# Adding minus the mean on DVE instead of POOL, and later memory scores, in a two-layer encoder step

## The chip, the cores and the metric

The kernel runs on one core of a Trainium2 chip. Times are microseconds (us) of device time for one launch; the number quoted for a kernel is the median of its runs. The engines are PE (TensorE, the matrix engine), DVE (VectorE), ACT (ScalarE), POOL (GpSimd) and SP (SyncE, which here only issues transfers).

## The reference, cut to what matters

One step of an encoder with two layers, for 256 prompt tokens and 64 sample tokens, 2048 features each, in fp32. Both layers also attend with 4 heads into 256 memory tokens.

```python
def layer_norm(x, g, b):
    mu = jnp.mean(xf, axis=-1, keepdims=True)
    var = jnp.mean(jnp.square(xf - mu), axis=-1, keepdims=True)
    y = (xf - mu) * lax.rsqrt(var + LN_EPS) * g + b

def mem_attend(q, mk, mv):
    s = jnp.einsum('bthd,bmhd->bhtm', q, mk) / math.sqrt(HEAD_DIM)
    p = jax.nn.softmax(s, axis=-1)
    return jnp.einsum('bhtm,bmhd->bthd', p, mv)

for layer in range(DEPTH):
    # layer 0: short convolution; layer 1: stick-breaking attention over one shared K and V
    main = ...
    mo = mem_attend(q_m, mem_k[layer], mem_v[layer])
    mix = jnp.concatenate([main, mo], axis=-1) @ w_out[layer]
    x = layer_norm(ALPHA * x + mix, ln_g[layer, 0], ln_b[layer, 0])
    f = jnp.square(jax.nn.relu(x @ w_ff1[layer])) @ w_ff2[layer]
    x = layer_norm(ALPHA * x + f, ln_g[layer, 1], ln_b[layer, 1])
```

## The kernel before

All 320 tokens lie on the free axis; features lie on the 128 partitions, as 16 feature tiles (`res`, the residual). Each product is made of panels of 256 output features (two tiles of 128). A panel's weights come in chunks of 4 feature tiles by 256 columns (512 KB), over SP's queue, into three buffers `raw`. For nearly full fp32 accuracy each factor is split into a rounded part and a rest: ACT casts `hi`, DVE subtracts `lo` (L126, L127), into five buffers each. PE then runs 24 matmuls for a chunk, three per feature tile and column tile: lo by xh, hi by xl, hi by xh (L172 to L174). `xh` and `xl` are the tokens' two parts. A quarter panel is the 12 matmuls of a chunk and one column tile.

Three of the four layer norms lie between two products: norm 0 before layer 0's feed-forward, norm 1 before layer 1's input product, norm 2 before layer 1's feed-forward. (The fourth, the output's, is written by another function, `write`, which the change leaves alone.) The product that follows such a norm does not wait for the mean and the deviation. Its first gemm, of two panels at once (four tiles, 8 chunks, all four accumulators `acc` in PSUM), runs on un-normalised tokens with two more columns (322 wide), and its four sums are finished afterwards: `finished` (L406 to L414) copies two columns (`wgb`, ACT), adds mneg times wgb (L412, DVE, which reads `acc` and so frees it), and multiplies by rstd (L413). Meanwhile `normalise` (L391 to L404) makes the true normalised tokens for all later gemms, four feature tiles at a time in four turns c0 to c3: add mneg on POOL (L399), multiply by rstd on DVE (L400), scale and shift tile by tile on ACT (L402), then split into `xh` and `xl` (L126, L127). `finish` (L352 to L371) makes mneg (ACT, L361) and, in three DVE instructions, rstd (L369 to L371).

In layer 1 the four tiles of the first gemm are the memory attention's four queries. `in_b` finishes them (L627, L628) and calls `mem_attend`, which puts three stages into a list: scores, turn and values. The stages are run one by one between quarter panels by `tick`; `later` says from which quarter panel on:

```python
    def later(gap, fn):
        stages.append((now[0] + 2, gap, fn))
```

The order on each engine is not simply the program's: a scheduler places instructions of all stages by its own estimate, and each engine then runs its list strictly in order.

Of the kernel before, what the change touches and what calls it, by code (L numbers as in the profile page):

```python
# [14 lines left out]
ALU = mybir.AluOpType  # L15
# [3 lines left out]
DM = 2048          # model width  # L19
KT = DM // P       # feature tiles  # L20
TP, TS = 256, 64   # prompt and sample tokens
T = TP + TS
DFF = 8192
NM = 256           # memory tokens
NMH = 4            # memory heads
DMEM = NMH * P
NH = 12            # main heads / main feature tiles
PAST = 512
CW = 256           # columns of a weight chunk
CK = 4             # feature tiles of a weight chunk  # L30
NKC = KT // CK
AFTER = (2, 3, 4, 5)   # chunks of the next products, after which their factors are normalised
CUTS = (0, 1, CK)   # pieces of the first chunks
# [7 lines left out]
def encoder_step(  # L41
    ctx: ExitStack,
    tc: tile.TileContext,
    xT: bass.AP,       # [P, KT, T]
    memT: bass.AP,     # [NKC, P, CK, NM]
    w_in_a: bass.AP,   # [20, NKC, P, CK, CW]
    w_in_b: bass.AP,
    w_mem: bass.AP,    # [2, 4, NKC, P, CK, CW]
    w_out: bass.AP,    # [2, 8, NKC, P, CK, CW]
    w_ff1: bass.AP,    # [2, 32, NKC, P, CK, CW]  # L50
    w_ff2: bass.AP,    # [2, 8, 4 * NKC, P, CK, CW]
    ck: bass.AP,       # [NH, P, PAST]
    cv: bass.AP,       # [NH, P, 4, P]
    cmk: bass.AP,      # [2, P, NMH, NM]
    cmv: bass.AP,      # [2, P, 2, DMEM]
    conv_w: bass.AP,   # [P, NH, 3]
    state: bass.AP,    # [P, NH, 2]
    ln_g: bass.AP,     # [P, 4, KT]
    ln_b: bass.AP,
    y_out: bass.AP,    # [P, KT, T]  # L60
    conv_out: bass.AP,  # [P, NH, 2, 2]
    k_out: bass.AP,    # [NH, P, T]
    v_out: bass.AP,    # [NH, P, T]
    mk_out: bass.AP,   # [2, NMH, P, NM]
    mv_out: bass.AP,   # [2, 2, P, DMEM]
# [12 lines left out]
    # Exp, Ln and every simple function in one table  # L78
    nc.scalar.preload_act_table_set("natural_log_exp_and_others")

# [8 lines left out]
    # mask[s, t]: 0 where s < t, BIG elsewhere  # L89
# [8 lines left out]
    # ntri[s', s] = -1 where s' >= s  # L98
# [30 lines left out]
    def load_split(jobs, cuts=(0, CK)):  # L129
        """jobs: (source, hi, lo) of chunks; loaded and split up to each cut of their feature tiles in turn."""  # L130
        raws = [wpool.tile([P, CK, CW], F32, name="raw", bufs=3) for _ in jobs]
        for a, b in zip(cuts[:-1], cuts[1:]):
            for raw, (src, hi, lo) in zip(raws, jobs):
                nc.sync.dma_start(out=raw[:, a:b, :], in_=src[:, a:b, :])
            for raw, (src, hi, lo) in zip(raws, jobs):
                split(hi[:, a:b, :], lo[:, a:b, :], raw[:, a:b, :])
# [9 lines left out]
    # stages of attention, run one by one between the products of the next tiles  # L146
# [3 lines left out]
    def later(gap, fn):  # L150
        """fn, at least gap quarter panels after the last stage (and one after this)."""
        stages.append((now[0] + 2, gap, fn))
# [7 lines left out]
    def gemm(panels, ah, al, on_tile, width=T, after=None):  # L160
        """panels: lists of chunk sources, worked on together; on_tile(i, j, psum); after(chunk)."""
        accs = [[pacc.tile([P, 512], F32, name="acc") for _ in range(CW // P)] for _ in panels]
        n = len(panels[0])
        for c in range(n):
            for i, panel in enumerate(panels):
                hi, lo = chunk(panel[c])
                for j in range(CW // P):
                    acc = accs[i][j][:, :width]
                    cols = slice(j * P, (j + 1) * P)
                    for k in range(CK):  # L170
                        kt = c * CK + k
                        mm(acc, lhsT=lo[:, k, cols], rhs=ah[:, kt, :width], start=kt == 0, stop=False)  # L172
                        mm(acc, lhsT=hi[:, k, cols], rhs=al[:, kt, :width], start=False, stop=False)  # L173
                        mm(acc, lhsT=hi[:, k, cols], rhs=ah[:, kt, :width], start=False, stop=kt == n * CK - 1)  # L174
                    if c == n - 1:
                        on_tile(i, j, acc)
                    tick()
            if after:
                after(c)

# [1 line left out]
    def mem_kv(layer, values, between=None):  # L182
        """The keys of the four heads, or the values."""
# [37 lines left out]
    def wk():  # L221
        """The pool of a phase's small tiles, in the place of the last phase's."""
        if phases:
            phases.pop().close()
        phases.append(ExitStack())
        ctx.callback(phases[-1].close)
        return phases[-1].enter_context(tc.tile_pool(name="work", bufs=2))
# [8 lines left out]
    def mem_attend(h, qm, mixh, mixl, turns):  # L236
# [40 lines left out]
        later(1, scores)  # L277
# [4 lines left out]
    class Norm:  # L282
        """Of r = factor * res + the last products, as they come. The next products begin on g * (r - c) (in xh and
        xl, with g and b as two more columns), and their sums are finished with the mean and the deviation."""
# [19 lines left out]
        def add(self, m, acc):  # L304
            """The last product for feature tile m: res[m] * factor + acc."""
            f = self.factor
            if m < 4:
                nc.vector.scalar_tensor_tensor(out=res[:, m, :], in0=res[:, m, :], scalar=f, in1=acc,
                                               op0=ALU.mult, op1=ALU.add)
                if m == 3:  # L310
                    self.center()
                return
            nc.vector.tensor_tensor(out=res[:, m, :], in0=acc, in1=res[:, m, :], op=ALU.add)  # L313
            last = m == KT - 1
            sq = work.tile([P, T], F32, name="sq")
            nc.scalar.activation(sq, res[:, m, :], AF.Square)  # L316
            if not last:
                nc.vector.tensor_tensor(out=self.s1, in0=self.s1, in1=res[:, m, :], op=ALU.add)
                nc.vector.tensor_tensor(out=self.s2, in0=self.s2, in1=sq, op=ALU.add)
            self.ahead(m)  # L320
            if last:
                self.finish(sq)

        def center(self):
            """c: the mean of the first 4 * P features, by which all are shifted."""
# [26 lines left out]
        def finish(self, sq):  # L352
# [10 lines left out]
            # var + eps: the shift keeps the mean below sqrt(3) deviations, so it stays above 0  # L363
# [4 lines left out]
            # one Newton step of 1 / sqrt(var)  # L368
# [6 lines left out]
        def write(self):  # L375
            """The normalised tokens are the result: the tiles shared among the engines."""
# [14 lines left out]
        def normalise(self, _):  # L391
            """Four feature tiles, a while after the first products have had theirs."""
            self.turn += 1
            if self.turn not in AFTER:
                return
            c = AFTER.index(self.turn)
            s = slice(c * CK, (c + 1) * CK)
            r = res[:, s, :]
            nc.gpsimd.tensor_tensor(out=r, in0=r, in1=mneg.unsqueeze(1).to_broadcast([P, CK, T]), op=ALU.add)  # L399
            nc.vector.tensor_tensor(out=r, in0=r, in1=rstd.unsqueeze(1).to_broadcast([P, CK, T]), op=ALU.mult)  # L400
            for m in range(c * CK, (c + 1) * CK):
                nc.scalar.activation(res[:, m, :], res[:, m, :], AF.Identity, bias=lb[:, self.idx, m:m + 1],  # L402
                                     scale=lg[:, self.idx, m:m + 1])
            split(xh[:, s, :T], xl[:, s, :T], r)  # L404

        def finished(self, acc, tag="qT"):  # L406
            """The product with the normalised tokens, without W' b; and W' b."""
# [125 lines left out]
    def stick_z(h, d):  # L533
# [4 lines left out]
        def z():  # L538
            # prompt in (keys 0, tokens 0), (keys 1, tokens 1), (keys 0, tokens 1); sample by key block
# [14 lines left out]
            # n = softplus(z) = max(z, 0) + ln(1 + exp(-|z|))  # L554
# [9 lines left out]
            # sums over the later key blocks of the sample  # L564
# [13 lines left out]
    def stick_a(h, d):  # L578
# [4 lines left out]
        def turn():  # L583
            # values with the keys on the partitions
# [8 lines left out]
        def sums():  # L593
            # log a = z - (sum of n over this key and the later ones)
# [30 lines left out]
    def in_b(m, acc):  # L625
        if m < NMH:
            qm, wb = norm.finished(acc, ("qT", "qT", "npr", "nsm")[m])  # L627
            nc.vector.tensor_scalar(out=qm, in0=qm, scalar1=wb, scalar2=QSCALE, op0=ALU.add, op1=ALU.mult)  # L628
            mem_attend(m, qm, mixh, mixl, 2)
# [30 lines left out]
def _panels(w):  # L660
    """[K, N] -> [N / CW, K / (CK * P), P, CK, CW]"""
    k, n = w.shape
    return np.ascontiguousarray(w.reshape(k // (CK * P), CK, P, n // CW, CW).transpose(3, 0, 2, 1, 4))
# [59 lines left out]
```

## Time and profile before

| what | value |
|---|---|
| median of 3 runs | 2850.72 us (2850.52 to 2853.23) |
| span of the profiled execution, first to last instruction | 2849.1 us |
| PE busy | 2801.0 us, 98% of the span |
| DVE busy | 1443.8 us, 51% |
| ACT busy | 1121.9 us, 39% |
| POOL busy | 86.6 us, 3% |
| granted PE clock, mean | 0.993 of full speed |
| mean traffic | 150 GB/s |

The profiled execution's own time is not listed apart from its span; the three runs lie 1.4 to 4.1 us above that span. A matmul of 320 columns is recorded as 0.31 us long, while the next one starts 0.15 us after it: PE's spans overlap, so its idle time is best read from the distance of two starts. In a timeline a row gives start, duration, engine, line, what is written and read, and in brackets the idle time before it with what ended it.

### The profile page before, as it was taken

What the parts mean: (1) busy time and instruction counts of PE and PEld (TensorE: products, weight loads), DVE (VectorE), ACT (ScalarE), POOL (GpSimd) and SP (SyncE); (2) the same over time, 40 slices, a digit from 0 to 9 for tenths busy, and PEclk for the clock granted to TensorE, in tenths of its full rate; (3) what the DMA queues carried; (4) which work ended last, traced back from release to release, by engine and by line L of the source; (5) the groups of instructions that cost most, each with busy time, mean ns of one, the idle gap of its engine ahead of it and who ended that gap; (6) DMA issues with size and microseconds to landing.
All of it is one profiled execution on the core that took longest, in us unless ns stands there. A gap on an engine that the chain in (4) does not pass through costs nothing.

```text
span 2849.1 us, 45960 instructions
## 1 busy us (share of the span) xinstructions
PE 2801.0 (98%) x19432; PEld 2773.9 (97%) x19432; DVE 1443.8 (51%) x1924; ACT 1121.9 (39%) x1537; POOL 86.6 (3%) x101
## 2 busy tenths in 40 slices
PE   8999999999999999999989999999999999999996
PEld 8999999999999999999989999999999999999996
DVE  5454457744444454445674444566444444444465
ACT  5433334543333243334454444445323333433333
POOL 1000000100000000000010000000000000000001
PEclk9999999999999999999999999999999999999998
DMA  8545555455555454554534545454544554555542
GB/s 295 179 127 148 150 153 149 126 150 154 149 149 150 152 149 148 150 153 142 155 110 150 152 152 157 123 154 137 152 149 148 151 151 149 148 150 152 150 148 89
DMA packets 118111, 427.52 MB, mean 150 GB/s; under 512 B 13761, under 2 KB 14321, under 8 KB 117905
## 3 DMA queue, kind: packets, MB, share of 16 engines
q1 hardware_dynamic: 113904, 412.14, 48.3%
q0 software_dynamic: 4000, 12.45, 1.3%
q8 instruction: 152, 2.49, 0.4%
q14 instruction: 55, 0.44, 0.0%
HBM read 415.86 MB, written 8.68 MB: 149 GB/s over the span
## 4 chain that ended last, share of the span: by engine, by line
PE 96%; DVE 1%; ACT 1%; DMA 1%; issue 0%; SPq 0%; ACTq 0%; DVEq 0%
PE acc L172 30%; PE acc L174 30%; PE acc L173 30%; DMA raw<-w_mem 1%; PE acc L206 1%; PE acc L205 1%; PE acc L204 1%; PE acc L200 0%; PE acc L202 0%; PE acc L201 0%; ACT hi L126 0%; PE zs L243 0%; ACT xh L126 0%; ACT res L402 0%; PE av L616 0%; DVE lo L127 0%
## 5 line engine op out<-in xcount | busy, mean ns | idle before, releaser
L127 DVE TENSOR_TENSOR lo<-raw,hi 128x1024 fp32r<-128x1024 f32 (+1 forms) x769 | 940.6, 1224 | 1209.2 <-ACT hi L126 1207.8
L126 ACT CAST hi<-raw 128x1024 fp32r<-128x1024 f32 (+1 forms) x769 | 805.4, 1047 | 1359.5 <-PE acc L174 1273.3
L172 PE MATMUL acc<-xh,lo 128*128 128x320 f32 (+1 forms) x3328 | 1036.5, 311 | 9.3 <-DVE fin L412 9.3
L174 PE MATMUL acc<-xh,hi 128*128 128x320 f32 (+1 forms) x3328 | 1033.5, 311 | 0.0
L173 PE MATMUL acc<-xl,hi 128*128 128x320 f32 (+1 forms) x3328 | 1029.7, 309 | 0.0
L174 PE MATMUL acc<-mh,hi 128*128 128x320 f32 x2560 | 792.1, 309 | 0.0
L172 PE MATMUL acc<-mh,lo 128*128 128x320 f32 x2560 | 791.3, 309 | 0.0
L173 PE MATMUL acc<-ml,hi 128*128 128x320 f32 x2560 | 791.0, 309 | 0.0
L172 PEld LDWEIGHTS acc<-xh,lo 128*128 128x128 f32 x3328 | 628.0, 189 | 14.0 <-DVE fin L412 10.3
L174 PEld LDWEIGHTS acc<-xh,hi 128*128 128x128 f32 x3328 | 628.5, 189 | 2.5 <-issue 2.3
L173 PEld LDWEIGHTS acc<-xl,hi 128*128 128x128 f32 x3328 | 627.7, 189 | 0.9 <-issue 0.4
L172 PEld LDWEIGHTS acc<-mh,lo 128*128 128x128 f32 x2560 | 480.6, 188 | 0.4
L174 PEld LDWEIGHTS acc<-mh,hi 128*128 128x128 f32 x2560 | 480.6, 188 | 0.3
L173 PEld LDWEIGHTS acc<-ml,hi 128*128 128x128 f32 x2560 | 480.6, 188 | 0.0
L126 ACT CAST mh<-rs 128x320 fp32r<-128x320 f32 x128 | 58.9, 460 | 58.5 <-DVE rs L436 58.4
L127 DVE TENSOR_TENSOR ml<-rs,mh 128x320 fp32r<-128x320 f32 x128 | 62.5, 489 | 31.6 <-ACT mh L126 31.6
L399 POOL TENSOR_TENSOR res<-res,mneg 128x1280 f32<-128x1280 f32 x12 | 37.4, 3142 | 1134.4 <-ACT mneg L361 1134.4
L436 DVE TENSOR_TENSOR rs<-rl 128x320 f32<-128x320 f32 x128 | 62.4, 489 | 8.0 <-ACT rl L434 8.0
L443 DVE SCALAR_TENSOR_TENSOR res<-res,acc 128x320 f32<-128x320 f32 x96 | 46.5, 484 | 39.2 <-PE acc L174 39.2
L434 ACT ACTIVATE rl<-acc 128x320 f32<-128x320 f32 x120 | 52.4, 437 | 32.9 <-PE acc L174 30.7
L200 PE MATMUL acc<-memh,lo 128*128 128x256 f32 x128 | 38.8, 303 | 9.3 <-DVE lo L127 9.3
L316 ACT ACTIVATE sq<-res 128x320 f32<-128x320 f32 x48 | 22.5, 469 | 59.5 <-DVE res L313 59.5
(208 smaller groups left out, 1256.8 us busy)
## 6 DMA issues: line engine op xcount, KB each, us to landing
raw<-w_ff SPq DMA_DIRECT2D x512, 512.0 KB, 3.6
raw<-w_in_a SPq DMA_DIRECT2D x80, 512.0 KB, 3.6
raw<-w_in_b SPq DMA_DIRECT2D x80, 512.0 KB, 3.6
raw<-w_out SPq DMA_DIRECT2D x64, 512.0 KB, 3.6
raw<-w_mem SPq DMA_DIRECT2D x31, 512.0 KB, 4.8
ckT<-ck POOLq DMA_DIRECT2D x12, 256.0 KB, 3.2
cvS<-cv POOLq DMA_DIRECT2D x12, 256.0 KB, 3.3
res<-xT SPq DMA_DIRECT2D x4, 640.0 KB, 6.3
```

The lines of the kernel that those rows point to most:

```text
L126: nc.scalar.copy(hi, src)
L127: nc.vector.tensor_tensor(out=lo, in0=src, in1=hi.bitcast(F32), op=ALU.subtract)
L172: mm(acc, lhsT=lo[:, k, cols], rhs=ah[:, kt, :width], start=kt == 0, stop=False)
L173: mm(acc, lhsT=hi[:, k, cols], rhs=al[:, kt, :width], start=False, stop=False)
L174: mm(acc, lhsT=hi[:, k, cols], rhs=ah[:, kt, :width], start=False, stop=kt == n * CK - 1)
L200: mm(acc, lhsT=wl[:, k, cols], rhs=mh[:, k, :], start=first, stop=False)
L204: mm(acc, lhsT=ml[:, k, cols], rhs=wh[:, k, :], start=first, stop=False)
L205: mm(acc, lhsT=mh[:, k, cols], rhs=wl[:, k, :], start=False, stop=False)
L399: nc.gpsimd.tensor_tensor(out=r, in0=r, in1=mneg.unsqueeze(1).to_broadcast([P, CK, T]), op=ALU.add)
L434: nc.scalar.activation(r, acc, AF.Relu)
L436: nc.vector.tensor_tensor(out=s, in0=r, in1=r, op=ALU.mult)
L443: nc.vector.scalar_tensor_tensor(out=res[:, m, :], in0=res[:, m, :], scalar=ALPHA if g == 0 else 1.0, in1=acc, op0=ALU.mult, op1=ALU.add)
```

## The change

Two edits, and comments removed (which makes no instruction different). In `normalise` the add of mneg is issued on DVE instead of POOL: 4 instructions of 128x1280 elements at each of norms 0, 1 and 2. In `mem_attend` the scores' stage gets a lag of its own, 4 quarter panels in layer 1 instead of 2; layer 0 keeps 2.

```diff
-    def later(gap, fn):
-        stages.append((now[0] + 2, gap, fn))
+    def later(gap, fn, lag=2):
+        stages.append((now[0] + lag, gap, fn))
...
-    def mem_attend(h, qm, mixh, mixl, turns):
+    def mem_attend(h, qm, mixh, mixl, turns, lag=2):
...
-        later(1, scores)
+        later(1, scores, lag)
         later(3, turn)
         later(1, values)
...
             r = res[:, s, :]
-            nc.gpsimd.tensor_tensor(out=r, in0=r, in1=mneg.unsqueeze(1).to_broadcast([P, CK, T]), op=ALU.add)
+            nc.vector.tensor_tensor(out=r, in0=r, in1=mneg.unsqueeze(1).to_broadcast([P, CK, T]), op=ALU.add)
             nc.vector.tensor_tensor(out=r, in0=r, in1=rstd.unsqueeze(1).to_broadcast([P, CK, T]), op=ALU.mult)
...
-            mem_attend(m, qm, mixh, mixl, 2)
+            mem_attend(m, qm, mixh, mixl, 2, 4)
```

DVE's list at norm 0, from the variance on (var, msq and rstd are the norm's; res is the residual; lo a chunk's rest; xl the tokens' rest; fin a finished sum), before:

```order
L364 SCALAR_TENSOR_TENSOR var<-zs,msq 128x320
L369 SCALAR_TENSOR_TENSOR msq<-r_5174 128x320
L370 TENSOR_TENSOR var<-msq,var 128x320
L371 SCALAR_TENSOR_TENSOR rstd<-var,r_5174 128x320
L400 TENSOR_TENSOR res<-res,rstd 128x1280
L127 TENSOR_TENSOR lo<-raw,hi 128x1024
L400 TENSOR_TENSOR res<-res,rstd 128x1280 x2
L127 TENSOR_TENSOR lo<-raw,hi 128x1024
L127 TENSOR_TENSOR xl<-res,xh 128x4x320
L400 TENSOR_TENSOR res<-res,rstd 128x1280
```

and now:

```order
L364 SCALAR_TENSOR_TENSOR var<-zs,msq 128x320
L399 TENSOR_TENSOR res<-res,mneg 128x1280
L369 SCALAR_TENSOR_TENSOR msq<-r_5174 128x320
L399 TENSOR_TENSOR res<-res,mneg 128x1280
L370 TENSOR_TENSOR var<-msq,var 128x320
L399 TENSOR_TENSOR res<-res,mneg 128x1280
L371 SCALAR_TENSOR_TENSOR rstd<-var,r_5174 128x320
L127 TENSOR_TENSOR lo<-raw,hi 128x1024
L400 TENSOR_TENSOR res<-res,rstd 128x1280 x2
L127 TENSOR_TENSOR lo<-raw,hi 128x1024
L400 TENSOR_TENSOR res<-res,rstd 128x1280
L399 TENSOR_TENSOR res<-res,mneg 128x1280
```

Three of the four adds stand between the steps of rstd, and a chunk's lo goes ahead of the first multiplication; the lists of norms 1 and 2 change in the same way up to here.

ACT's list at norm 0, the part that ends with the first copy of wgb (hi a chunk's rounded part, xh the tokens'), before:

```order
L126 CAST xh<-res 128x4x320
L402 ACTIVATE res<-res,lgb 128x320
L126 CAST hi<-raw 128x1024
L402 ACTIVATE res<-res,lgb 128x320 x2
L126 CAST hi<-raw 128x1024
L402 ACTIVATE res<-res,lgb 128x320 x2
L126 CAST xh<-res 128x4x320
L126 CAST hi<-raw 128x1024
L409 COPY wgb<-acc 128x2 x2
```

and now, from the two hi behind Exp on:

```order
L126 CAST hi<-raw 128x1024 x2
L402 ACTIVATE res<-res,lgb 128x320 x5
L126 CAST xh<-res 128x4x320
L402 ACTIVATE res<-res,lgb 128x320 x3
L126 CAST hi<-raw 128x1024
L126 CAST xh<-res 128x4x320
L402 ACTIVATE res<-res,lgb 128x320 x4
L126 CAST hi<-raw 128x1024 x2
L402 ACTIVATE res<-res,lgb 128x320
L126 CAST xh<-res 128x4x320
L402 ACTIVATE res<-res,lgb 128x320
L409 COPY wgb<-acc 128x2
```

The first copy of wgb now stands ahead of the last two scalings, behind 14 of the 16 and behind three casts of xh, as before; before, all 16 stood ahead of it.

PE's list where layer 1's first gemm ends (322 wide) and the next begins (320 wide), with the first memory head's scores (L243; zs, zp are their places in PSUM, fin its finished query, mk_sb and smk the memory keys of prompt and sample), before:

```order
L172 MATMUL acc<-xh,lo 128x322
L243 MATMUL zs<-mk_sb,fin 128x256
L243 MATMUL zp<-mk_sb,fin 128x256
L173 MATMUL acc<-xl,hi 128x322
L174 MATMUL acc<-xh,hi 128x322
L172 MATMUL acc<-xh,lo 128x322
L173 MATMUL acc<-xl,hi 128x322
L174 MATMUL acc<-xh,hi 128x322
L172 MATMUL acc<-xh,lo 128x322
L173 MATMUL acc<-xl,hi 128x322
L174 MATMUL acc<-xh,hi 128x322
L243 MATMUL zs<-smk,fin 64x256
```

and now:

```order
L172 MATMUL acc<-xh,lo 128x322
L173 MATMUL acc<-xl,hi 128x322
L174 MATMUL acc<-xh,hi 128x322
L243 MATMUL zs<-mk_sb,fin 128x256
L243 MATMUL zp<-mk_sb,fin 128x256
L172 MATMUL acc<-xh,lo 128x320
L173 MATMUL acc<-xl,hi 128x320
```

The first two scores stand 8 matmuls later, at the very end of the first gemm; the third, which stood right behind that end, now follows 19 matmuls of the next gemm. SP's list is the same in both.

## Rows read from the trace of the kernel before

**Rows 1.** The page's first lines: span, busy time of each engine.

```profile
span 2849.1 us, 45960 instructions
...
PE 2801.0 (98%) x19432; PEld 2773.9 (97%) x19432; DVE 1443.8 (51%) x1924; ACT 1121.9 (39%) x1537; POOL 86.6 (3%) x101
```

**Rows 2.** PE's waits: who waited for whom, us in total, times, longest.

```profile
PE acc L172 <- DVE fin L412: 9.3, 4, 3.8
...
PE zs L243 <- DVE fin L628: 7.3, 1, 7.3
```

**Rows 3.** Waits of PE's weight loads, same columns.

```profile
PEld zs L243 <- ACT p L248: 1.3, 6, 0.3
```

**Rows 4.** Timeline of PE at the end of norm 0's first gemm.

```profile
548.67 0.30 PE L174 MATMUL acc<-xh,hi 128*128 128x322 f32 x1
552.74 0.41 PE L172 MATMUL acc<-xh,lo 128*128 128x320 f32 x1 [3.77 <-DVE fin L412]
```

**Rows 5.** Timeline of PE near the end of norm 1's first gemm.

```profile
1458.56 0.31 PE L174 MATMUL acc<-xh,hi 128*128 128x322 f32 x1
1458.71 0.32 PE L172 MATMUL acc<-xh,lo 128*128 128x322 f32 x1
```

**Rows 6.** Stretches behind the waits; the third number from the right is PEclk.

```profile
550.00:560.00 10.00, 7.09 (x36) 6.84 (x36) 9.23 (x14) 7.17 (x15) 0.00 (x0) 0.83 0.63 183
1466.30:1476.30 10.00, 9.95 (x46) 8.24 (x47) 7.71 (x19) 4.31 (x13) 0.00 (x0) 0.74 0.35 105
1945.00:1955.00 10.00, 6.63 (x34) 6.63 (x35) 8.96 (x14) 7.18 (x14) 0.00 (x0) 0.83 0.65 199
```

**Rows 7.** Timeline of POOL at norm 0.

```profile
520.73 12.45 POOL L399 TENSOR_TENSOR res<-res,mneg 128x1280 f32<-128x1280 f32 x4 [115.78 <-ACT mneg L361]
```

**Rows 8.** Timeline of DVE from norm 0's variance to its first finished sum.

```profile
520.82 0.48 DVE L364 SCALAR_TENSOR_TENSOR var<-zs,msq 128x320 f32<-128x320 f32 x1
522.35 1.72 DVE L369 SCALAR_TENSOR_TENSOR msq<-r 128x320 f32<-128x320 f32 x1 [1.04 <-ACT r L367]
524.10 3.13 DVE L370 TENSOR_TENSOR var<-msq,var 128x320 f32<-128x320 f32 x1
527.26 3.12 DVE L371 SCALAR_TENSOR_TENSOR rstd<-var,r 128x320 f32<-128x320 f32 x1
530.48 4.06 DVE L400 TENSOR_TENSOR res<-res,rstd 128x1280 f32<-128x1280 f32 x1
...
535.60 2.88 DVE L400 TENSOR_TENSOR res<-res,rstd 128x1280 f32<-128x1280 f32 x2
538.40 1.21 DVE L127 TENSOR_TENSOR lo<-raw,hi 128x1024 fp32r<-128x1024 f32 x1
539.54 1.48 DVE L127 TENSOR_TENSOR xl<-res,xh 128x1280 fp32r<-128x1280 f32 x1
...
552.15 0.54 DVE L412 SCALAR_TENSOR_TENSOR fin<-mneg,wgb,acc 128x320 f32<-128x320 f32 x1
```

**Rows 9.** Timeline of POOL at the last norm (function write).

```profile
2827.33 5.12 POOL L380 TENSOR_TENSOR res<-res,mneg 128x320 f32<-128x320 f32 x5 [898.50 <-ACT mneg L361]
```

**Rows 10.** Timeline of DVE at the last norm.

```profile
2832.72 0.48 DVE L370 TENSOR_TENSOR var<-msq,var 128x320 f32<-128x320 f32 x1
...
2833.52 0.48 DVE L371 SCALAR_TENSOR_TENSOR rstd<-var,r 128x320 f32<-128x320 f32 x1
```

**Rows 11.** Timeline of ACT at norm 0: scalings, casts, first copies of wgb.

```profile
534.57 2.30 ACT L402 ACTIVATE res<-res,lgb 128x320 f32<-128x320 f32 x4 [9.51 <-DVE res L400]
536.78 1.04 ACT L126 CAST hi<-raw 128x1024 fp32r<-128x1024 f32 x1
537.72 1.28 ACT L126 CAST xh<-res 128x1280 fp32r<-128x1280 f32 x1
...
551.56 0.21 ACT L409 COPY wgb<-acc 128x2 f32<-128x2 f32 x2
```

**Rows 12.** Timeline of DVE at norm 1: the first query finished.

```profile
1465.82 0.38 DVE L628 TENSOR_SCALAR fin<-fin,wgb 128x320 f32<-128x320 f32 x1
```

## The prediction

> **What bounds the kernel now.** I read the page's head first: PE is busy for 98% of the span [rows 1], so only what keeps PE waiting or slow can move the time. Next I read PE's waits [rows 2]. Two entries matter: PE's matmuls wait four times, 9.3 us in all, for DVE's finished sums (fin, L412), which free the accumulators, and once, 7.3 us, for the first memory query (fin, L628). The timelines place them: two at norm 0 (the longer is [rows 4]), two alike at norm 2, and the long one at norm 1, when PE stands in front of the first scores, 16 matmuls into the last chunk of the gemm [rows 5]. A start follows a start after 0.15 us in undisturbed work [rows 5], while a matmul is recorded as 0.30 long, so each of the five waits costs some 0.15 more than its entry: 548.67 to 552.74 less 0.15 is 3.92, and the entry is 3.77 [rows 4]. The five waits are 16.6 + 5 x 0.15 = 17.4 us.
>
> They cost more than that, as the windows behind them show [rows 6]: the granted clock averages 0.83 over 10 us behind norm 0's long wait, 0.83 behind norm 2's, and 0.74 behind norm 1's. [...] In all three cases PE had stood still before the clock fell. Waits and clock together: **23.4 us**, all of it at three of the four norms.
>
> **Why DVE and ACT are late there.** At norm 0 POOL's four adds run back to back from 520.73 for 12.45 us, 3.1 each [rows 7]. Beside them DVE's msq takes 1.72, var 3.13, rstd 3.12 and the first multiplication 4.06 us [rows 8]. At the last norm POOL's adds end at 2832.45 [rows 9], and right after it var and rstd take 0.48 each [rows 10], on tiles of the same size. So the long ones are not the price of the work: a DVE instruction that overlaps an add on POOL ends with it, and three small instructions in a row cost three adds. Only the first multiplication needs an add's result at all. From 522.35 to 534.54 DVE does what else would take about 0.5 + 0.5 + 0.5 + 1.4, or 2.9 us: 9 us are lost. ACT pays for it, standing idle for 9.51 us until that multiplication is done [rows 11]; behind it lie 16 scalings and the casts, and so the first wgb comes at 551.56 [rows 11] and fin at 552.15 [rows 8].
>
> **The change, part by part.** *The adds.* POOL loses three times 12.45 us; nothing behind them on POOL is wanted at that time. DVE gains 12 adds. No add of that shape on DVE is in the trace; the nearest rows are L400, the same shape, types and broadcast operand: two in 2.80 us from start to start, 1.40 each, and 1.48 for the longest reading [rows 8]. The bounds are 1.40, and 3.1 if an add cost on DVE what it cost on POOL. I take 1.40: same engine, same bytes.
>
> Now DVE's new list at norm 0, with steps of 0.4 for var and 0.46 for msq and rstd (0.54 less the overlap): variance to 521.2, add c0 522.6, msq 523.1, add c1 524.5, var 524.9, add c2 526.3, rstd 526.7, lo 527.9 (1.14, the step from 538.40 to 539.54 [rows 8]), multiplication c0 529.3, c1 530.7, lo 531.8, c2 533.2, add c3 534.6, xl 536.0, lo 537.2, c3 538.6. Before, c0 was done at 534.5, c1 and c2 by 538.4 [rows 8]. So DVE, although it does 5.6 us more, hands ACT its first work **5.2 us earlier**.
>
> ACT's list from there, with 0.55 for a scaling (2.21 for four), 0.94 for hi and 1.2 for xh [rows 11]: five scalings and xh 533.3, three scalings, hi and xh 537.0, four scalings and two hi 541.1, scaling, xh and scaling 543.4, wgb 543.6. (PE allows that: tile 0's sums end three quarter panels, 36 x 0.15 = 5.4 us, ahead of the end of the gemm at 548.8.) DVE's xl for that xh ends at 544.4, and fin at 544.9. PE asks for the accumulator at 548.8: nearly 4 us to spare. If ACT kept its old list, its 17.0 us from 534.57 to 551.56 would merely start 5.2 earlier: fin ends at 547.5, still in time. The second wait there, for the fourth fin, was at most 0.9 (9.3 less two of 3.8, over two) and goes with the same shift. Norm 2 has the same lists. Gain: 2 x (3.92 + 1.04 + 1.7) = 13.3 us.
>
> *Norm 1.* L628 ended at 1466.2 [rows 12]. By the shift of fin at norm 0 (552.15 to 544.4, 7.7 us) it ends at 1458.5, by DVE's 5.2 alone at 1461.0. PE stood ready at 1458.9 [rows 5].
>
> *The later scores.* PE's work is the same; its first two scores stand 8 matmuls later, so PE asks at 1458.71 + 9 x 0.15 = 1460.1. By the count nothing waits; by the worse bound 0.9 us are left. Of the 10.1 us lost at norm 1 (7.5 waiting, 2.6 by the clock) the adds alone would save 7 to 10, and the later scores at most the last 1.2. What is queued behind the scores on PE is the weights' matmuls; what follows from them is that the softmax, the transposes and the first stick-breaking head come one or two quarter panels later (1.8 us each), beside matmuls of the panels, which don't need them. The one place that can show a new wait is the third score: it takes zs again, which ACT's exponential must have read, and ACT stands there behind xh c3, which itself must wait for the end of the first gemm. Such waits were 1.3 us for six in the kernel before, 0.3 at most [rows 3]; the ends are 0 and 1.3, and I take 0.7.
>
> **Sum.** 23.4 - 0.7 = 22.7 us. From the span of 2849.1 that leaves 2826.4; the median stood 1.6 above that span, so **2828.0 us**.
>
> **Rivals.** *First, the score wait stays in part.* For it: at norm 1 DVE's list puts a chunk's lo and two more sums ahead of the first L628, and each lo waits for its cast. Against it: those casts have their buffers by then. If the query came at 1463.8, PE would wait some 3.8 us and the clock fall as it did behind the 3.8 us of norm 0: 3.8 + 1.7, or 2833.5 us; if nothing at all were gained at norm 1, 2838.1. It decides when L628 ends later than 1460.1.
>
> *Second, slower: the adds lengthen DVE's list.* If DVE's long steps came from something else than POOL (their operands, say), they would stay, and 4 x 1.40 = 5.6 us would come on top, at three norms. For it: DVE was busy for 9.23 of 10 us behind norm 0's wait [rows 6] and POOL for 3% of the span [rows 1], so work goes from an idle engine to the one that is late. The price: 3 x 5.6 = 16.8, and another 1.7 us at half clock behind each, some 5: 2872 us. It decides by whether var (L370) still takes over 3 us with POOL empty; the last norm [rows 9, 10] says no. [...]
>
> *Third, no change:* ACT, not DVE, decides when fin comes, and its 16 scalings and casts take up the 5.2 us. Then the waits stay within a few us of what they are, and the time within 0.2% (5.7 us, about what a measurement can tell from no change): 2848. Against it: ACT's 9.51 us of idle time [rows 11] end with DVE's multiplication.
>
> **Chances.** The forecast 0.80, the first rival 0.13, the second 0.03, the third 0.04. Both of the first are faster by over 0.2%: 0.93 in all; same 0.04; slower 0.03. The range reaches from 2825.5 (no new wait, 2827.3, less 1.8 for the scatter of 2.7 us between runs) to 2838 (nothing gained at norm 1). An add at 3.1 us on DVE would put multiplication c0 at 534.4 instead of 529.3, which is the third rival's place.
>
> **What the changed profile would show.** Right: var and rstd at 0.5 us at norms 0 to 2; POOL's busy time down by 37 us to 49; the adds at 1.4 to 1.5 us; no PE wait on fin over 1 us; the granted clock 1.00 over the three stretches; DVE's busy time down, by 3 x 9 for the stretched steps against 12 x 1.48 added, to about 1435. Wrong: L370 or L371 still near 3 us; PE still waiting for L412 or L628; a new wait of PE on ACT's exponential or on a weight chunk, with the clock falling behind it.

## The result, and the profile after

The changed kernel takes 2827.77 us (median of 4 runs, 2826.41 to 2828.56) against 2850.62 us for the kernel before (4 runs): the ratio is 0.9918, with a 95% interval of 0.9906 to 0.9930. The forecast was 2828.0. The execution profiled took 2827.72 us, 1.7 above its span.

The page's head, where [rows 1] stood before (busy time, share of the span, instructions):

```profile
span 2826.0 us, 45944 instructions
...
PE 2792.7 (99%) x19432; PEld 2767.3 (98%) x19432; DVE 1432.4 (51%) x1936; ACT 1122.9 (40%) x1537; POOL 49.4 (2%) x89
```

DVE, with twelve instructions more, is busy for 11 us less, and POOL for 37 us less. PE's waits, where [rows 2] stood (total, times, longest):

```profile
PE acc L200 <- DVE lo L127: 11.0, 5, 4.7
```

There is no other entry. This one belongs to the start-up and stood in the kernel before too, with 9.3 us; both entries of [rows 2] are gone. Where the time came from is read from one instruction that each norm has once, the variance (L364), in DVE's timeline; first the kernel before, norms 1 and 2 and the output's (norm 0's, at 520.82, is the first of [rows 8]):

```profile
1432.05 0.48 DVE L364 SCALAR_TENSOR_TENSOR var<-zs,msq 128x320 f32<-128x320 f32 x1
...
1916.46 0.48 DVE L364 SCALAR_TENSOR_TENSOR var<-zs,msq 128x320 f32<-128x320 f32 x1
...
2827.10 0.49 DVE L364 SCALAR_TENSOR_TENSOR var<-zs,msq 128x320 f32<-128x320 f32 x1 [1.73 <-PE zs L358]
```

and the changed kernel, from norm 0 on:

```profile
521.09 0.48 DVE L364 SCALAR_TENSOR_TENSOR var<-zs,msq 128x320 f32<-128x320 f32 x1
...
1425.61 0.48 DVE L364 SCALAR_TENSOR_TENSOR var<-zs,msq 128x320 f32<-128x320 f32 x1
...
1900.08 0.48 DVE L364 SCALAR_TENSOR_TENSOR var<-zs,msq 128x320 f32<-128x320 f32 x1
...
2804.00 0.49 DVE L364 SCALAR_TENSOR_TENSOR var<-zs,msq 128x320 f32<-128x320 f32 x1 [1.73 <-PE zs L358]
```

| stretch | before | after | gain |
|---|---|---|---|
| start to norm 0 | 520.82 | 521.09 | -0.3 |
| norm 0 to norm 1 | 911.23 | 904.52 | 6.7 |
| norm 1 to norm 2 | 484.41 | 474.47 | 9.9 |
| norm 2 to the last norm | 910.64 | 903.92 | 6.7 |
| last norm to the end of the span | 22.0 | 22.0 | 0 |

The sum is 23.1 us, the difference of the two spans; the three norms alone make 23.4 (unrounded). The first stretch holds nothing that was changed: up to the same instruction it took from 519.64 to 522.24 us in the runs below whose lists agree up to there, so its -0.3 is scatter. DVE's timeline at norm 0, where [rows 8] stood, shows how:

```profile
521.49 1.48 DVE L399 TENSOR_TENSOR res<-res,mneg 128x1280 f32<-128x1280 f32 x1
522.89 0.48 DVE L369 SCALAR_TENSOR_TENSOR msq<-r 128x320 f32<-128x320 f32 x1
523.29 1.48 DVE L399 TENSOR_TENSOR res<-res,mneg 128x1280 f32<-128x1280 f32 x1
524.70 0.48 DVE L370 TENSOR_TENSOR var<-msq,var 128x320 f32<-128x320 f32 x1
525.10 1.49 DVE L399 TENSOR_TENSOR res<-res,mneg 128x1280 f32<-128x1280 f32 x1
526.50 0.48 DVE L371 SCALAR_TENSOR_TENSOR rstd<-var,r 128x320 f32<-128x320 f32 x1
526.90 1.22 DVE L127 TENSOR_TENSOR lo<-raw,hi 128x1024 fp32r<-128x1024 f32 x1
528.04 2.88 DVE L400 TENSOR_TENSOR res<-res,rstd 128x1280 f32<-128x1280 f32 x2
...
544.89 0.54 DVE L412 SCALAR_TENSOR_TENSOR fin<-mneg,wgb,acc 128x320 f32<-128x320 f32 x1
```

msq, var and rstd take 0.48 us each instead of 1.72, 3.13 and 3.12, and an add on DVE 1.48 (1.40 from start to start). ACT's first scaling and first wgb, where [rows 11] stood:

```profile
529.56 2.84 ACT L402 ACTIVATE res<-res,lgb 128x320 f32<-128x320 f32 x5 [0.66 <-DVE res L400]
...
543.92 0.16 ACT L409 COPY wgb<-acc 128x2 f32<-128x2 f32 x1
```

ACT's idle 9.51 us have become 0.66. The first fin ends at 545.43 (544.89 + 0.54), and PE takes up the next gemm without a break, here in PE's timeline, where [rows 4] stood:

```profile
548.94 0.31 PE L174 MATMUL acc<-xh,hi 128*128 128x322 f32 x1
549.09 0.31 PE L172 MATMUL acc<-xh,lo 128*128 128x320 f32 x1
```

At norm 1 the first query is finished by DVE at 1451.86 + 0.38 (first row; [rows 12] before), and PE reaches the scores at 1453.60, 0.14 us behind the matmul before them (the two rows of its timeline):

```profile
1451.86 0.38 DVE L628 TENSOR_SCALAR fin<-fin,wgb 128x320 f32<-128x320 f32 x1
```

```profile
1453.46 0.30 PE L174 MATMUL acc<-xh,hi 128*128 128x322 f32 x1
1453.60 0.59 PE L243 MATMUL zs<-mk_sb,fin 128*128 128x256 f32 x2
```

The windows behind norms 0, 1 and 2 (same columns as [rows 6]) now show a granted clock of 1.00 throughout:

```profile
550.00:560.00 10.00, 10.00 (x70) 10.00 (x70) 9.55 (x15) 6.50 (x14) 0.00 (x0) 1.00 0.44 128
1453.60:1463.60 10.00, 10.00 (x65) 9.01 (x64) 9.52 (x21) 5.02 (x12) 0.00 (x0) 1.00 0.38 115
1935.00:1945.00 10.00, 10.00 (x70) 10.00 (x70) 5.80 (x7) 3.51 (x4) 0.00 (x0) 1.00 0.69 209
```

In the kernel before, the windows of [rows 6] were made up of stretches at 1.00 and at 0.50, here behind norm 1's wait:

```profile
1468.00:1470.00 2.00, 2.00 (x8) 1.91 (x8) 1.57 (x5) 1.13 (x4) 0.00 (x0) 0.50 0.01 4
...
1472.00:1474.00 2.00, 2.00 (x17) 1.99 (x16) 1.21 (x5) 1.58 (x5) 0.00 (x0) 1.00 0.77 246
```

The waits of PE's weight loads on the memory heads' exponential, where [rows 3] stood:

```profile
PEld zs L243 <- ACT p L248: 1.4, 6, 0.3
```

### The profile page after: what moved, and what is told of

It is laid out like the page before. It is cut to its first block, busy times and chain, and to the rows that moved or that the text cites. A ratio compares the mean times of both kernels' runs of the same rounds, so it can differ in the third digit from the quotient of the medians.

```text
span 2826.0 us, 45944 instructions
## 1 busy us (share of the span) xinstructions
PE 2792.7 (99%) x19432; PEld 2767.3 (98%) x19432; DVE 1432.4 (51%) x1936; ACT 1122.9 (40%) x1537; POOL 49.4 (2%) x89
## 3 DMA queue, kind: packets, MB, share of 16 engines
q0 software_dynamic: 4000, 12.45, 1.3%
## 4 chain that ended last, share of the span: by engine, by line
PE 98%; DVE 1%; DMA 1%; ACT 0%; issue 0%; SPq 0%; ACTq 0%; DVEq 0%
PE acc L172 31%; PE acc L174 31%; PE acc L173 31%; DMA raw<-w_mem 1%; PE acc L206 1%; PE acc L205 1%; PE acc L204 1%; PE acc L200 0%; PE acc L202 0%; PE acc L201 0%; PE av L616 0%; PE zs L243 0%; DVE res L381 0%; PE av L269 0%; DVE res L380 0%; PE zs L552 0%
## 5 line engine op out<-in xcount | busy, mean ns | idle before, releaser
L200 PEld LDWEIGHTS acc<-memh,lo 128*128 128x128 f32 x128 | 25.7, 201 | 12.2 <-DVE lo L127 12.2
```

The source lines that it names most:

```text
L200: mm(acc, lhsT=wl[:, k, cols], rhs=mh[:, k, :], start=first, stop=False)
```

## The experiments

Two questions were put. Which of the two edits brings the 23 us? And was POOL in the way because it made the sums late, because it was busy at all, or because its instructions collide with DVE's? The theory is the prediction's: a DVE instruction that overlaps an add on POOL is held until that add ends. In the runs that put lines into `finish`, the lines behind it are numbered higher (L404 is the add L399, L374 to L376 are L369 to L371, L417 is L412, L633 is L628). Ratios are to the kernel before, beside which each group of runs was timed.

### Each edit alone

The adds on DVE, the scores as before:

```diff
-            mem_attend(m, qm, mixh, mixl, 2, 4)
+            mem_attend(m, qm, mixh, mixl, 2)
```

> The adds on DVE, the scores' lag at 2 as before. PE's list has the first two scores 6 matmuls (0.9 us) earlier than in the changed kernel. Theory (the adds carry nearly all of it): the query is finished at 1452.2 in the changed kernel's trace and PE would ask at about 1452.7, so no wait or one under 1 us, no stretch at the lower clock: 2827 to 2829.5 us. Rival (the later scores are what frees norm 1): 10 us stay at norm 1, 2838 us.

Measured: 2828.06 us, ratio 0.9921 (0.9906 to 0.9935). PE has no wait on fin, the clock averages 0.997 over the span as in the changed kernel (0.993 before), and norm to norm the three stretches are those of the changed kernel to within 0.2 us (904.53, 474.59 and 903.92). At norm 1 the first query is finished at 1451.82 and PE reaches the scores at 1452.30, so 0.48 us were to spare without the later scores. This edit alone brings all of it.

The scores later, the adds on POOL:

```diff
-            nc.vector.tensor_tensor(out=r, in0=r, in1=mneg.unsqueeze(1).to_broadcast([P, CK, T]), op=ALU.add)
+            nc.gpsimd.tensor_tensor(out=r, in0=r, in1=mneg.unsqueeze(1).to_broadcast([P, CK, T]), op=ALU.add)
```

> The adds on POOL, the scores' lag at 4. Theory: norms 0 and 2 as before (waits 3.8 and 0.9, the lower clock behind them); at norm 1 PE asks 8 matmuls later and waits some 6.1 instead of 7.3 us, the clock falls all the same: 2849.4 us, 1.2 under the kernel before. Rival (the lag frees norm 1): 2840.5 us.

Measured: 2849.75 us, ratio 0.9997 (0.9987 to 1.0006). PE's waits:

```profile
PE acc L172 <- DVE fin L412: 8.4, 3, 3.8
...
PE zs L243 <- DVE fin L628: 6.1, 1, 6.1
```

The wait at the scores is 6.1 instead of 7.3 us: the later scores do what their 8 matmuls are worth, 1.2 us, and in the time (1.3 us between the medians) that is within the scatter. With the adds on DVE there is nothing left for them to save.

### POOL beside, for nobody

The changed kernel, with the same adds of the same size on POOL again, into a tile that nobody reads:

```diff
             nc.scalar.mul(mneg, m1, -1.0)
+            if not self.last:
+                idle = work.tile([P, CK, T], F32, name="idle", bufs=1)
+                mb = mneg.unsqueeze(1).to_broadcast([P, CK, T])
+                for _ in range(4):
+                    nc.gpsimd.tensor_tensor(out=idle, in0=mb, in1=mb, op=ALU.add)
```

> The changed kernel, and beside it POOL again adds four times 128x1280 from mneg on, at norms 0 to 2, into a tile that nobody reads. DVE's list is that of the changed kernel word for word. Theory (an add on POOL holds up DVE's instructions that overlap it, whoever needs its result): for 12.45 us DVE gets through one instruction per POOL add, the first multiplication ends near 537 instead of 529.5, PE waits some 4 us at norms 0 and 2 and 6 at norm 1, the clock falls: 2843 to 2856 us. Rival (POOL mattered as the late maker of the sums): no step of DVE is longer, 2827.8 us.

Measured: 2851.02 us, ratio 0.9998 (0.9989 to 1.0008): the whole gain is gone, though nobody needs POOL's result and the lists of PE, DVE and ACT are the changed kernel's. POOL's and DVE's timelines at norm 0:

```profile
521.84 11.93 POOL L366 TENSOR_TENSOR idle<-mneg 128x1280 f32<-128x1280 f32 x4 [115.79 <-ACT mneg L361]
```

```profile
522.33 3.21 DVE L404 TENSOR_TENSOR res<-res,mneg 128x1280 f32<-128x1280 f32 x1
525.46 2.61 DVE L374 SCALAR_TENSOR_TENSOR msq<-r 128x320 f32<-128x320 f32 x1
527.99 3.60 DVE L404 TENSOR_TENSOR res<-res,mneg 128x1280 f32<-128x1280 f32 x1
531.52 2.60 DVE L375 TENSOR_TENSOR var<-msq,var 128x320 f32<-128x320 f32 x1
534.04 1.48 DVE L404 TENSOR_TENSOR res<-res,mneg 128x1280 f32<-128x1280 f32 x1
535.45 0.48 DVE L376 SCALAR_TENSOR_TENSOR rstd<-var,r 128x320 f32<-128x320 f32 x1
```

Up to POOL's end at 533.77 DVE gets through one instruction per add, 2.6 to 3.6 us each, small or large; the very next add takes 1.48 and rstd 0.48. An instruction so held does nearly all of its own work after POOL's: the second and the fourth of POOL's adds end at 527.72 and 533.77, msq and var 0.35 us behind them (0.48 is their time alone), and the two adds on DVE 1.35 us behind the first and the third (1.48 alone). PE's waits are back at the changed kernel's own places:

```profile
PE acc L172 <- DVE fin L417: 7.7, 2, 3.8
PE zs L243 <- DVE fin L633: 6.3, 1, 6.3
```

This is the run that decides against the rival of late sums.

### What on POOL collides

Two runs took the same place with other work for POOL: fills, which read nothing (after one small pass over mneg, so that they start then), and a multiplication with one operand instead of an add's two.

```diff
+            if not self.last:
+                idle = work.tile([P, CK, T], F32, name="idle", bufs=1)
+                nc.gpsimd.tensor_scalar(out=idle[:, 0, :], in0=mneg, scalar1=1.0, scalar2=None, op0=ALU.mult)
+                for _ in range(12):
+                    nc.gpsimd.memset(idle, 0.0)
```

> The changed kernel, and at norms 0 to 2, from mneg on, POOL fills a tile that nobody reads 12 times (128x1280, about 14 us), after one small pass over mneg that makes it start then. DVE's list is that of the changed kernel. Theory (what holds DVE's two-input instructions up is POOL's reading of its operands in SBUF): a fill reads nothing, DVE's steps keep 0.48 and 1.48 us, 2827 to 2829 us. Rival (any instruction on POOL holds DVE up): as the run with POOL's adds beside, 2850 us, or less by the shorter fills, 2835 to 2851.

Measured: 2827.13 us, ratio 0.9915 (0.9901 to 0.9930), as the changed kernel. POOL's timeline, and in DVE's one of the steps in the midst of the fills:

```profile
521.71 14.69 POOL L366 MEMSET idle<- 128x1280 f32 x12
```

```profile
524.29 0.48 DVE L375 TENSOR_TENSOR var<-msq,var 128x320 f32<-128x320 f32 x1
```

So with the others there: msq, var and rstd take 0.48 to 0.49 us, the adds 1.48 to 1.49. A POOL that is busy for 14.69 us without reading costs DVE nothing. The one-operand run:

```diff
+            if not self.last:
+                idle = work.tile([P, CK, T], F32, name="idle", bufs=1)
+                mb = mneg.unsqueeze(1).to_broadcast([P, CK, T])
+                for _ in range(4):
+                    nc.gpsimd.tensor_scalar(out=idle, in0=mb, scalar1=1.0, scalar2=None, op0=ALU.mult)
```

> The changed kernel, and at norms 0 to 2, from mneg on, POOL multiplies mneg (read four times over, 128x1280) by one into a tile that nobody reads, four times: one input instead of an add's two. DVE's list is that of the changed kernel. Theory (reading in SBUF is enough, one operand or two): DVE's steps that overlap it end with it, so the delay follows the length of these instructions, which no row shows; if they take 1.5 to 3 us each, 2830 to 2851 us and DVE's msq, var and adds above 1.5 us beside them. Rival (only two operands collide): DVE's steps unchanged, 2827.8 us.

Measured: 2857.51 us, ratio 1.0022 (1.0013 to 1.0031), slower than the kernel before and above the range given, because these instructions are longer than was allowed for, 4.2 us each. PE waits 8.0 us for fin, 6.4 for the first query and 5.9 for chunks' lo. POOL's timeline, and DVE's at the second add and at var:

```profile
522.15 16.89 POOL L366 TENSOR_SCALAR idle<-mneg 128x1280 f32<-128x1280 f32 x4 [115.79 <-ACT mneg L361]
```

```profile
529.65 1.48 DVE L404 TENSOR_TENSOR res<-res,mneg 128x1280 f32<-128x1280 f32 x1
531.06 3.28 DVE L375 TENSOR_TENSOR var<-msq,var 128x320 f32<-128x320 f32 x1
```

One operand is enough to collide: msq, var and rstd take 3.28 us each. The expectation that the adds on DVE would be long too held for the first only (3.89 us); the other two take 1.48 beside POOL, and there it is POOL that is longer. Its shortest, median and longest instruction (ns) in this run, and the same for the adds that POOL did for nobody:

```profile
L366 POOL TENSOR_SCALAR idle<-mneg x12: 3477/4322/4525, 522.2 to 1933.6; 128x1280 f32<-128x1280 f32 x12
L366 POOL TENSOR_TENSOR idle<-mneg x12: 2346/2948/3453, 521.8 to 1924.8; 128x1280 f32<-128x1280 f32 x12
```

In both runs the long ones of norm 0 are those that begin while an add on DVE is still running. Side by side: DVE's adds, msq and var took 2.6 to 3.6 us where POOL's adds held them, msq, var and rstd 3.28 each beside one-operand work, and 0.48 to 0.49 beside fills, for which POOL reads nothing. What the two engines get in each other's way over, no run here shows.

No run varied the number of DVE's operands, two in each of those held above. The kernel before has one row that bears on it, at the last norm, beside a multiplication of 128x320 on POOL:

```profile
2838.59 0.98 DVE L383 TENSOR_SCALAR res<-res,lgb 128x320 f32<-128x320 f32 x1
```

It reads one tile (lgb gives a number for each partition), and the other three of its kind take 0.44 us. So two tile operands on DVE may not be needed for the delay; whether this is the same collision is not shown.

### POOL's adds in pieces

The kernel before, each add cut by feature tile:

```diff
-            nc.gpsimd.tensor_tensor(out=r, in0=r, in1=mneg.unsqueeze(1).to_broadcast([P, CK, T]), op=ALU.add)
+            for m in range(c * CK, (c + 1) * CK):
+                nc.gpsimd.tensor_tensor(out=res[:, m, :], in0=res[:, m, :], in1=mneg, op=ALU.add)
```

> The kernel before, with each of POOL's adds cut into four of 128x320 (16 at each norm, of about 0.8 to 1.05 us). Theory (a DVE instruction waits for the end of the POOL instruction that it overlaps, so the size of POOL's instruction is what counts): msq, var and rstd take about 1 us each instead of 1.7 to 3.1, the first multiplication ends near 527.5, the waits of norms 0 and 2 go, at norm 1 up to 2 us stay: 2827 to 2833 us, although POOL does the same work. Rival (POOL's whole busy time or its results hold DVE up): the steps stay at about 3 us or the multiplication waits until 534, 2848 to 2852 us.

Measured: 2843.68 us, ratio 0.9972 (0.9962 to 0.9983), between the two, so neither expectation held to the end. DVE's timeline at norm 0 (in this run L400 is the add, L401 the multiplication):

```profile
523.29 1.05 DVE L370 TENSOR_TENSOR var<-msq,var 128x320 f32<-128x320 f32 x1
524.38 1.05 DVE L371 SCALAR_TENSOR_TENSOR rstd<-var,r 128x320 f32<-128x320 f32 x1
525.53 1.99 DVE L401 TENSOR_TENSOR res<-res,rstd 128x1280 f32<-128x1280 f32 x1
...
535.54 2.15 DVE L401 TENSOR_TENSOR res<-res,rstd 128x1280 f32<-128x1280 f32 x1 [2.44 <-POOL res L400]
```

The first half came as expected: var and rstd take 1.05 us, and the first multiplication ends at 527.52, sooner than in the changed kernel. Then DVE holds up POOL in turn. The pieces' shortest, median and longest time (ns), and all 16 of norm 0:

```profile
L400 POOL TENSOR_TENSOR res<-res,mneg x48: 864/1126/2139, 521.2 to 1930.8; 128x320 f32<-128x320 f32 x48
```

```profile
521.16 21.17 POOL L400 TENSOR_TENSOR res<-res,mneg 128x320 f32<-128x320 f32 x16 [115.80 <-ACT mneg L361]
```

A piece that meets one of DVE's long instructions takes 2.13 instead of 0.88 us, the 16 take 21.17 us where four large adds took 12.45, and the later multiplications wait for them (2.44 us at 535.54). PE waits six times for fin, 6.2 us in all, and 4.7 us for the first query.

### Twice the adds on DVE

The changed kernel, with the four idle adds on DVE (`nc.vector` in the third run's lines):

> The changed kernel, and DVE adds four times more at each of norms 0 to 2, 128x1280 from mneg into a tile that nobody reads: 5.6 us more of DVE in the same stretch. DVE's list runs these between the steps of rstd and the true adds behind it; one true add moves behind the first finished sum. Theory (DVE has slack of nearly 4 us at norm 0 and 1 us at norm 1, and only what exceeds it is paid): the first multiplication ends 2.7 us later than in the changed kernel, waits of 0 to 2 us come back at norm 1, the clock stays up: 2828 to 2832 us. Rival (DVE's own list is the bound, each of its us counts): three times 5.6, 2844.5 us.

Measured: 2831.77 us, ratio 0.9931 (0.9914 to 0.9948). 5.6 us more work on DVE at each of three norms cost 4 us in all. The size was as expected, the place was not: PE does not wait for fin or for the query, but twice for a chunk's lo, about 8 us into the gemm that follows norms 0 and 2, where DVE's backlog reaches the weights:

```profile
PE acc L172 <- DVE lo L127: 1.9, 2, 1.0
```

The two profiled executions are 4.6 us apart. By PE's first matmul of each norm's gemm, 0.7 of it lies ahead of norm 0, where none of the added adds has run, and 1.2, 1.4 and 1.2 behind norms 0, 1 and 2. The two waits shown make up nearly all of the 1.2 at norms 0 and 2; at norm 1 two waits of 0.3 us on the memory heads' softmax are found, and the rest stays open.

## Why the prediction was right

- **Where the time was lost.** The 23.4 us of waits and lower clock at three norms were the whole stake, and 23.4 came back there: 6.7, 9.9 and 6.7 where the text had 6.7, 10.1 and 6.7. The span fell by 23.1, since the start-up was 0.3 longer. The clock's part of the stake, 1.7, 2.6 and 1.7 us, is what the windows of [rows 6] fall short of 1.00, times their 10 us. No run shows the clock as a frequency; what the kernel before shows is 0.50 of full speed, with 320-wide matmuls starting 0.27 us apart instead of 0.15 (at norm 0 from 553.5 to 556.5).
- **Why DVE was late.** The last norm's two rows [rows 9, 10] carried the argument, and the run with POOL's adds for nobody shows it by itself: 2851.02 us with the changed kernel's lists. The prediction's words, that an overlapped DVE instruction ends with POOL's add, are not exact: it ends later by nearly its own time. At norm 0 of the kernel before msq, var and rstd end 0.35 us behind POOL's first three adds, and the first multiplication 1.36 behind the fourth (533.18 by [rows 7], 534.54 by [rows 8]). The 9 us were read from the rows and don't hang on it. The words are also only half of the matter: POOL was held by DVE as well, in pieces and beside DVE's adds.
- **The adds at 1.40 us.** Measured 1.48, and 1.40 from start to start; the upper bound of 3.1 was not in play. (It was a time beside DVE, too: the shortest add of that shape on POOL took 2.35.)
- **The lists counted out.** Scalings from 529.3 (529.56), wgb at 543.6 (543.92), end of fin 544.9 (545.43), PE's request 548.8 (549.09, with the start 0.3 later). At norm 1 the query was 1.4 us ahead of the request; by the count it was 1.6.
- **The later scores.** Worth 1.2 us at most was right as a bound; alone they took 1.2 us off the wait and 1.3 off the median, inside the interval, and beside the adds nothing.
- **The 0.7 us for the third score** is the one term that was mis-sized. Waits of PE's weight loads on that exponential came to 1.4 us in six, as the 1.3 of [rows 3], so the change added nothing there. That the median came within 0.2 us of the forecast is in part luck: the 0.7 did not occur, the start-up was 0.3 longer, and the changed kernel's own runs lie 2.2 us apart.
- **The rivals.** The second falls with var's 0.48 us, the third with ACT's idle 0.66, the first with the missing wait on L628. Twice the adds, 2831.77 us, shows in addition that DVE's length was not the bound there: of 5.6 us more on DVE, PE lost 1.2 to 1.4 at each norm.

## What to carry to other kernels

When small DVE instructions take as long as whatever runs on POOL beside them (var 3.13 us here, beside adds of 3.0 to 3.2), count POOL's work as DVE's: moving it onto DVE can shorten DVE, which was busy for 11 us less with twelve adds more. Compare the same instruction where POOL is idle (var 0.48) before costing it, and look at what POOL's instruction reads, since fills did no harm here (var 0.48 beside them). In this kernel PE's waits at phase boundaries, 17.4 us, were paid for again behind the long ones at the lower clock, 0.83, 0.74 and 0.83 over 10 us, so price both from the rows.

## What the runs showed that was not expected

- The collision works in both directions: POOL's 128x320 add took 0.88 us, and 2.13 when it met a 128x1280 instruction of DVE. Smaller pieces on POOL traded DVE's delay for POOL's.
- On POOL a one-operand multiplication of 128x1280 took 3.48 us at the least, more than the 2.35 of the shortest two-operand add. With what DVE's adds put on top it was 4.2 on average, and the kernel was slower than the one before by 0.22%.
- In the kernel before the clock fell to 0.50 in or behind PE's waits of 3.8 us and more at the norms. Of the runs that brought these waits back, POOL's adds for nobody show 0.83 over 10 us at norm 0 (554 to 564); over the span that run averages 0.993, the later scores alone and the one-operand run 0.994, against 0.997 in the changed kernel. The run in pieces shows a lower clock too at its 4.7 us for the first query, 0.66 over 10 us (second row). Behind its waits at norm 0, at most 1.6 us each, the clock stayed at 1.00 (first row):

```profile
555.00:565.00 10.00, 8.45 (x56) 8.19 (x57) 9.13 (x16) 7.31 (x14) 0.00 (x0) 1.00 0.47 130
1460.00:1470.00 10.00, 8.40 (x36) 6.97 (x37) 7.59 (x20) 5.28 (x13) 0.00 (x0) 0.66 0.44 142
```

- The length of a single wait does not decide it, though. In the start-up of the kernel before, the clock averaged 0.66 over 5 us around and behind a wait of 1.79 us (the two rows here); in the changed kernel it stayed at 1.00 there, behind one of 1.75 us. What made the difference is open.

```profile
30.34 0.39 PE L200 MATMUL acc<-memh,lo 128*128 128x256 f32 x1 [1.79 <-DVE lo L127]
30.00:35.00 5.00, 4.67 (x26) 4.67 (x27) 2.53 (x3) 3.37 (x4) 0.50 (x1) 0.66 0.68 237
```
